# A two-layer bidirectional encoder trunk: the global branch's output projection trails its gates by four feature tiles instead of three, and some attention steps move half a product earlier

## The chip, the cores and the metric

One Trainium2 (trn2) chip, one core. The metric is the device time of one execution in microseconds (us); it covers the whole trunk, from the load of the first activations to the last store. The kernel before took 846.28 us in the median of 3 runs (844.58 to 846.31). PE is TensorE, DVE is VectorE, ACT is ScalarE, POOL is GpSimd, SP is SyncE, which issues the loads.

## The reference

Two layers over 528 tokens (16 meta tokens and a grid of 8 rows of 64), width 1024. Each layer normalises the residual stream, projects it once, and runs two attentions on parts of the projection: a global one (GQA, 8 query heads on 2 key/value heads of 64) and a windowed one (NA, 8 heads, an 8 x 16 window with a learned bias and the meta keys). Each branch is gated, projected to the width, and the two are merged by sigmoid gates:

```python
def hybrid_layer(x, norm_g, w_in, q_norm_g, k_norm_g, rpb, w_o_attn, w_o_na, w_out, cos, sin):
    b, l, _ = x.shape
    h = rms_norm(x, norm_g)
    proj = jnp.einsum('bld,de->ble', h, w_in)
    qa, ka, va, za, qb, kb, vb, zb, ga, gb = split_cols(proj)
...
    oa = gqa_attention(qa, ka, va) * jax.nn.silu(za)
...
    ob = neighbourhood_attention(qb, kb, vb, rpb) * jax.nn.silu(zb)

    ya = jnp.einsum('ble,ed->bld', oa, w_o_attn)
    yb = jnp.einsum('ble,ed->bld', ob, w_o_na)
    mixed = jax.nn.sigmoid(ga) * ya + jax.nn.sigmoid(gb) * yb
    return x + jnp.einsum('bld,de->ble', mixed, w_out)
```

After the second layer the meta tokens are dropped.

## The kernel before, in words

Activations are kept transposed: features on the partitions, tokens along the free dimension, in 8 feature tiles. Every product is made in three passes over split operands (`product`, L325 to L327): weights and activations are each held as a rounded part (`hi`, fp32r) and the remainder (`lo`), and hi x hi, hi x lo and lo x hi are summed in a PSUM bank, named `pp` for a projection and `y` for the output projection of a branch. In layer 0 a product of one feature tile has two halves of 264 columns, 24 matmuls each; in layer 1 most have one half of 512 columns.

Weights stream in chunks of 512 columns: `weights` (L229 on) issues the load `raw` on SP, the cast `whi` on ACT (L240) and the remainder `wlo` on POOL (L241), four buffers of each, in the sequence of the list `order` (L207 to L220), three chunks ahead of their use. A chunk's name is layer, number, half: GA (26 to 33) are the gates of the global branch, GB (34 to 41) those of the window branch, WOA (42 to 45) and WOB (46 to 49) the branches' output projections, and 50 on the final one.

The two attentions run beside the projections. Each has a queue, `Side`, that `product` advances by a tick after each half product (in layer 1 also in the middle of one). A unit (GQA: one query head for two blocks of 128 queries, each with scores S of its own, so 16 units; `av_7_1` is the last) or a head (NA) may start at each fourth tick; its steps are then due so many ticks later, by the tables `GQA_AT` and `NA_AT`. In these, "split" are the two casts `pth` (ACT) and subtractions `ptl` (DVE) of a unit's transposed probabilities, which the matmuls `av` (L905) then read; "stages" are six steps of a head: preparation, scores Sb (L556, L557; reduced on DVE at L990), first transpositions ta and tm, second transpositions tb, third tc, and sums avb. "values" are two transpositions of the window's values, the second named vtc; they belong to the even heads, one for each pair. `split` (L190) makes hi and lo of a tile: `tah` and `tal` of ta, `oa_3a` and `oa_3b` of the gated output oa_3 of the global branch's last feature tile.

PSUM buffers: two for `pp` and `y`, two for transpositions (tag tp: ta, tb, tc, tm, vtc), and a single one of two banks, S, for scores of both attentions: the unit's scores (reduced at L837) and the window's Sb.

What is due at a tick is written into the instruction streams at that place; a scheduler then orders each engine's stream by its own priorities and the dependences, which is why the built order is read below.

After all projections come the merges. `merge_gate` makes a gate tile (L1131, L1132), `merge_half` the output projection of a branch (L1137 multiplies it by the gate). In the loop over m the product of tile m - LAG follows the gate of tile m, first for GB and WOB, then for GA and WOA; in the second loop the two branches are added (L1170) and split into `mx`. At m = LAG - 1 `side_gqa.finish()` (L1166) runs the ticks of the queue that are still open, since the product after it reads the last `oa`. In layer 1 the loop also starts the splits of the final weights (`last_split`, POOL L272).

Of the kernel before, what the change touches and what calls it, by code (L numbers as in the profile page):

```python
# [33 lines left out]
DEPTH = 2  # L34


GQA_AT = ({"scores": (0, 1), "turn": (1, 2), "back": 3, "split": (5, 5), "ends": 5, "divide": (2, 3, 6), "sums": (7, 7)},
          {"scores": (0, 1), "turn": (1, 2), "back": 3, "split": (5, 5), "ends": 5, "divide": (2, 3, 6), "sums": (7, 7)})
NA_AT = ({"stages": (0, 2, 5, 5, 5, 7), "values": (3, 4), "divide": (3, 4, 7)},
         {"stages": (0, 2, 4, 5, 5, 7), "values": (3, 4), "divide": (3, 4, 7)})  # L40

NORM_AT = ({"tokens": (0, 1, 3), "squares": (1, 1, 2, 3, 2), "heads": (2, 3, 5, 7, 6), "values": (1, 4)},
# [4 lines left out]
QA, KA, VA, ZA, QB, KB, VB, ZB, GA, GB = 0, 4, 5, 6, 10, 14, 18, 22, 26, 34  # L47
WOA, WOB, WOUT = 42, 46, 50
NCHUNK = 58

LAG = 3

# [41 lines left out]
def trunk_kernel(ctx: ExitStack, tc: tile.TileContext, xT, w, gn, gf, bias, rope, out):  # L96
    nc = tc.nc
# [15 lines left out]
    def slot(tag, name, dt=F32):  # L113
        n = NKEY if tag in ("KB", "KR", "K", "E") else NTOK
        t = slots.tile([P, n], dt, tag=tag, bufs=BUFS[tag], name=name)
        return t[:, :NTOK] if tag == "E" else t
# [90 lines left out]
    order = []  # L207
    for l in range(DEPTH):
        cols = [QA, QA + 1, QA + 2, QA + 3, KA, VA]
        for j in range(4):  # L210
            cols += [KB + j, QB + j, VB + j, ZB + j, ZA + j]
        order += [(l, c, i) for c in cols for i in range(2)]
        if l == 0:

            order = order[6:]
        for gate, wo in ((GB, WOB), (GA, WOA)):
            for m in range(8 + LAG):
                order += [(l, gate + m, 0), (l, gate + m, 1)] if m < 8 else []
                order += [(l, wo + (m - LAG) // 2, (m - LAG) % 2)] if m >= LAG else []
        order += [(l, WOUT + m, i) for m in range(8) for i in range(2)] if l < DEPTH - 1 else []  # L220
    place = {key: i for i, key in enumerate(order)}
    ready, loaded = [], []
# [44 lines left out]
    def last_split(us):  # L267
        for u in us:
            hi, lo = (((key_half if tag == "KB" else lambda name, dt: slot(tag, name, dt))(f"wl{u}{tag}", F32R))[:, :4 * P]
                      for tag in ("h", KEEP[u]))  # L270
            cast = nc.scalar.copy(hi, last_raw[u])
            sub = nc.gpsimd.tensor_sub(lo, last_raw[u], hi.bitcast(F32))  # L272
            split_at["weights"] = cast.ins, sub.ins
            last_w[u] = hi, lo

    l = 0
# [157 lines left out]
    first, ends = {}, ((0, HALF), (HALF, NTOK))  # L434
# [19 lines left out]
    for l in range(DEPTH):  # L454
        last = l == DEPTH - 1
# [135 lines left out]
        qs, turn = [], None  # L591
        for j in range(4):
# [3 lines left out]
            with tc.issue_after(evac["low"].ins):  # L596
                if l == 0 and j == 0:
                    turn = rotate
                else:
                    if turn:  # L600
                        turn()
                    turn = None
# [224 lines left out]
        zgate, oa, o_t, newest, sums_a = {}, [None] * 4, {}, {}, {}  # L827
# [19 lines left out]
        def global_unit(kv, parts, n, name, done):  # L847
# [7 lines left out]
            def scores(i):  # L855
                q, qs, scale, total = parts[i]
                if i == 0:
                    c["both"] = slots.tile([P, 2 * NTOK], F32, tag="M", bufs=BUFS["M"], name=f"P{name}")
                    c["p"] = [c["both"][:, NTOK * t:NTOK * (t + 1)] for t in range(len(parts))]
                softmax(c["p"][i], q, qs, kv, NMETA - first_token[i], n, scale, total, f"{name}_{i}")  # L860

            def turn(i):

                a, b = (0, NREAL) if i == 0 and len(parts) > 1 else (NREAL * i, NREAL * i + NREAL + 32)
                if len(parts) == 1:
                    nc.gpsimd.memset(c["both"][:n, NTOK:b], 0.0)
                nc.vector.transpose(c["both"][:n, a:b], c["both"][:n, a:b])  # L867
                if i == len(parts) - 1:
                    c["there"] = dpool.tile([P, 2 * (NREAL + 32)], F32, tag="turned", bufs=3, name=f"turn{name}")
                    nc.sync.dma_start(c["there"][:n, :b], c["both"][:n, :b])  # L870
# [30 lines left out]
            def sums(first, last):  # L901
                if first == 0:
                    c["av"] = bank(ps_a, f"av{name}", "avg")[:, :width]
                for i in range(first, last):
                    nc.tensor.matmul(c["av"], rows2(c["t"][i][0]), c["t"][i][1], start=i == 0, stop=i == 8)  # L905
                if last == 9:
                    done(c["av"])

            steps = [(at, lambda i=i: scores(i)) for i, at in zip(range(len(parts)), GQA_AT[l]["scores"])]
            for i, at in zip(range(len(parts)), GQA_AT[l]["turn"][-len(parts):]):  # L910
                steps.append((at, lambda i=i: turn(i)))
            steps.append((GQA_AT[l]["back"], back))
            n_t = 4 // per
            for i, (at, then) in enumerate(zip(GQA_AT[l]["split"][:n_t], GQA_AT[l]["sums"][-n_t:])):
                steps.append((at, lambda kt=per * i: split_part(kt)))
                f = 2 * per * (i + 1)
                steps.append((then, lambda a=2 * per * i, b=f + (f == 8): sums(a, b)))
            steps.append((GQA_AT[l]["ends"], split_ends))
            return sorted(steps, key=lambda x: x[0])
# [26 lines left out]
        def start_unit(hd, i):  # L946
# [6 lines left out]
            if g == 6:  # L953
                steps += zip(GQA_AT[l]["divide"], divided_later(sums_a[j], lambda: zgate[j], f"a{l}_{j}"))
            return sorted(steps, key=lambda x: x[0])
# [135 lines left out]
        def start_head(hd):  # L1091
            steps = list(zip(NA_AT[l]["stages"], windowed_head(hd)))
            j = hd // 2
            if hd % 2 == 0:
                steps += [(at, lambda i=i: window_values(j, i)) for i, at in enumerate(NA_AT[l]["values"])]
                kvq[j]["sums"] = tiny.tile([P, 8], F32, tag="sumb", name=f"sumb{l}_{j}")
            else:
                steps += zip(NA_AT[l]["divide"], divided_later(kvq[j]["sums"], lambda: zb[j], f"b{l}_{j}"))
            return sorted(steps, key=lambda x: x[0])
# [35 lines left out]
        def merge_half(m, t, c, br, out, spans=None):  # L1135
            for ps, a, b in product(l, c + m // 2, br, full, (m % 2,), f"y{m % 2}", spans):
                nc.vector.scalar_tensor_tensor(out[:, a:b], t[:, a:b], 1.0, ps, op0=ALU.add, op1=ALU.mult)  # L1137
                yield a, b

        mb, gates = [], {}  # L1140
        for m in range(8 + LAG):
            if m < 8:
                gates[m] = merge_gate(GB, m)
            if m == LAG - 1:
                side_na.finish()
                while ending:
                    ending.pop(0)()
            if m >= LAG:
                mb.append(slot("B", f"mb{l}_{m - LAG}"))
                for _ in merge_half(m - LAG, gates[m - LAG], WOB, ob, mb[m - LAG]):  # L1150
                    pass
        mixed = []
        for m in range(8 + LAG):
            if m < 8:
                gates[m] = merge_gate(GA, m)
            if last and m == 7:

                weights(l, WOA + 3, 1, 1)
                with tc.issue_after(split_at["gate"].ins):
                    last_split((0, 1, 2))  # L1160
            if m == LAG - 1:
                side_gqa.finish()
            if m >= LAG:
                ma = slot("G", f"ma{l}_{m - LAG}")
                hi, lo = two("M", f"mx{l}_{m}", F32R)
                end = m == 7 + LAG  # L1166
                for a, b in merge_half(m - LAG, gates[m - LAG], WOA, oa, ma):
                    if (end and full) or b == N:
                        a = a if end else 0
                        nc.vector.tensor_add(ma[:, a:b], ma[:, a:b], mb[m - LAG][:, a:b])  # L1170
                        with ExitStack() as held:
                            if last and m in (7, 8):
                                held.enter_context(tc.issue_after(split_at["weights"][0]))
                            split(hi[:, a:b], lo[:, a:b], ma[:, a:b])
                mixed.append((hi, lo))
                if last and m in (7, 8):
                    with tc.issue_after(split_at["hi"].ins):
                        last_split(((3, 4, 5), (6, 7))[m - 7])
            if last and m == 4:
                last_load(range(KT))  # L1180

# [37 lines left out]
    sums = tiny.tile([P, 50], F32, tag="mh", bufs=1, name="sums")  # L1219
    acc, ms, rx = sums[:, :12].rearrange("p (t i) -> p t i", i=3), sums[:, 12:16], sums[:, 16:20]  # L1220
    h2 = D // 4
    for f in range(2):
        for t in range(4):
            x = xs[f, t]
            end = f == 1 and t == 3
# [89 lines left out]
```

## Time and profile before

| | us |
|---|---|
| median of 3 runs | 846.28 (844.58 to 846.31) |
| the profiled execution | 845.68 |
| its span in the profile | 844.0 |
| PE busy | 821.0 (97%) |
| DVE, ACT, POOL busy | 522.8, 474.8, 422.8 |
| mean granted clock | 0.996 |

The span is the time between the profile's first and last instruction, 1.7 us less than the execution's own time. A matmul's busy time overlaps with that of the next, so that the distance of two starts tells what one costs. A wait is put down to the line and tile that released it.

### The profile page before, as it was taken

To read this page: it belongs to the slowest core of one execution; us is meant where nothing else is said; L and a number is where in the kernel's file an instruction comes from. 1 tells how busy PE (TensorE), PEld (TensorE's weight loads), DVE (VectorE), ACT (ScalarE), POOL (GpSimd) and SP (SyncE) were. 2 spreads that over 40 slices of the span, in tenths; PEclk is the share of its full clock that TensorE was granted. 3 is DMA by queue.
4 is the path that set the end of the run, shared out by engine and by line. 5 is a ranking of instruction groups with operands and counts; after the bars stand their busy time and mean duration, and the time that the engine had idled before them with its cause. 6 is when DMAs were issued, how large, how long until landed. Compare 5 with 4: busy or idle time off the path is not lost.

```text
span 844.0 us, 16154 instructions
## 1 busy us (share of the span) xinstructions
PE 821.0 (97%) x5662; PEld 757.9 (90%) x5662; DVE 522.8 (62%) x1152; ACT 474.8 (56%) x1137; POOL 422.8 (50%) x362
## 2 busy tenths in 40 slices
PE   9999999999999999899999999999999999999997
PEld 9999999999999999899998989898988787778786
DVE  7976667676765562436547656766776556545633
ACT  8654766667864563333445456675768545543422
POOL 1664545444444453654764644444545436464851
PEclk9999999999999999999999999999999999999999
DMA  7277564667454664335555585647566566444502
GB/s 277 89 195 223 133 196 116 197 195 197 147 161 118 188 178 128 108 93 150 151 141 121 152 212 154 196 160 225 153 187 197 167 193 187 140 147 140 185 3 101
DMA packets 113249, 135.00 MB, mean 160 GB/s; under 512 B 31888, under 2 KB 66192, under 8 KB 113168
## 3 DMA queue, kind: packets, MB, share of 16 engines
q1 hardware_dynamic: 112448, 132.90, 54.0%
q8 instruction: 45, 0.74, 0.4%
q10 hardware_dynamic: 720, 1.06, 0.3%
q14 instruction: 36, 0.29, 0.1%
HBM read 98.50 MB, written 21.84 MB: 143 GB/s over the span
## 4 chain that ended last, share of the span: by engine, by line
PE 85%; DVE 6%; ACT 3%; issue 2%; DMA 2%; SPq 1%; POOL 0%; POOLq 0%; DVEq 0%; ACTq 0%
PE pp L327 18%; PE pp L325 18%; PE pp L326 18%; PE av L905 4%; PE y L326 3%; PE y L327 3%; PE y L325 3%; DVE ptl L194 2%; PE avb L1052 2%; PE S L556 2%; PE S L557 2%; PE pf L1234 2%; PE pf L1236 2%; PE pf L1235 2%; PE tb L129 1%
## 5 line engine op out<-in xcount | busy, mean ns | idle before, releaser
L241 POOL TENSOR_TENSOR wlo<-raw,whi 128x512 fp32r<-128x512 f32 x210 | 287.5, 1376 | 322.2 <-ACT whi L240 262.1
L327 PE MATMUL pp<-hh,wlo 128*128 128x264 f32 (+3 forms) x1040 | 325.8, 313 | 0.6 <-POOL wlo L241 0.6
L325 PE MATMUL pp<-hh,whi 128*128 128x264 f32 (+3 forms) x1040 | 326.1, 314 | 0.3 <-DVE ma L1137 0.3
L326 PE MATMUL pp<-hl,whi 128*128 128x264 f32 (+3 forms) x1040 | 324.0, 312 | 0.0
L327 PEld LDWEIGHTS pp<-hh,wlo 128*128 128x128 f32 x1040 | 196.4, 189 | 11.2 <-POOL wlo L241 0.8
L326 PEld LDWEIGHTS pp<-hl,whi 128*128 128x128 f32 x1040 | 196.8, 189 | 9.5
L325 PEld LDWEIGHTS pp<-hh,whi 128*128 128x128 f32 x1040 | 196.2, 189 | 9.5 <-DVE ma L1137 0.5
L240 ACT CAST whi<-raw 128x512 fp32r<-128x512 f32 x210 | 128.7, 618 | 116.5 <-PE pp L326 41.4
L867 DVE STREAM_TRANSPOSE P<-P 128x512 f32<-128x512 f32 x64 | 46.4, 726 | 38.9 <-ACT P L841 38.6
L898 POOL TENSOR_TENSOR ga<-pm,ga 32x128 fp32r<-32x128 f32 x64 | 40.4, 632 | 47.9 <-issue 26.8
L194 DVE TENSOR_TENSOR ptl<-P,pth 128x512 fp32r<-128x512 f32 x64 | 55.6, 881 | 12.8 <-ACT pth L193 10.3
L1131 DVE TENSOR_TENSOR mg<-pp,rbc 128x264 f32<-128x264 f32 (+1 forms) x48 | 24.7, 515 | 50.2 <-PE pp L327 49.5
L837 DVE CUSTOM_DVE_ANT_1 P<-S,r 128x528 f32<-128x528 f32 x64 | 44.8, 700 | 14.5 <-PE S L557 13.7
L841 ACT ACTIVATE P<-P,st 128x528 f32<-128x528 f32 x64 | 47.1, 737 | 1.7
L1132 ACT ACTIVATE mg<-mg 128x264 f32<-128x264 f32 (+1 forms) x48 | 23.7, 493 | 36.9 <-DVE mg L1131 36.8
L193 ACT CAST pth<-P 128x512 fp32r<-128x512 f32 x64 | 39.2, 612 | 1.4 <-DMA P<-turn 1.3
L905 PE MATMUL av<-ptl,VA 128*128 128x256 f32 x128 | 35.0, 299 | 4.1 <-DVE ptl L194 3.7
L992 ACT ACTIVATE bias<-bias,stb 128x208 f32<-128x208 f32 (+1 forms) x64 | 31.0, 486 | 13.3 <-DVE stb L990 13.2
L326 PE MATMUL pp<-mx,whi 128*128 128x264 f32 x128 | 36.6, 286 | 0.0
L327 PE MATMUL pp<-mx,wlo 128*128 128x264 f32 x128 | 36.4, 284 | 0.0
L325 PE MATMUL pp<-mx,whi 128*128 128x264 f32 x128 | 36.3, 284 | 0.0
L840 ACT ACTIVATE st<-st 128x1 f32<-128x1 f32 x64 | 13.0, 202 | 40.9 <-DVE st L837 40.5
(534 smaller groups left out, 1727.4 us busy)
## 6 DMA issues: line engine op xcount, KB each, us to landing
raw<-in_w_dram SPq DMA_DIRECT2D x210, 256.0 KB
turn<-P SPq DMA_DIRECT2D x32, 528.0 KB
P<-turn SPq DMA_DIRECT2D x128, 128.0 KB
bias<-in_bias_dram SPq DMA_DIRECT2D x16, 480.0 KB
KB<-KB SPq DMA_DIRECT2D x24, 272.0 KB
rawl<-in_w_dram SPq DMA_DIRECT2D x16, 256.0 KB
x<-in_xT_dram SPq DMA_DIRECT2D x8, 264.0 KB
xr<-in_xT_dram SPq DMA_DIRECT2D x8, 264.0 KB
```

Source lines behind the costliest of these rows:

```text
L193: split_at["hi"] = nc.scalar.copy(hi, src)
L194: split_at["any"] = nc.vector.tensor_sub(lo, src, hi.bitcast(F32))
L240: cast = nc.scalar.copy(hi, raw)
L241: sub = nc.gpsimd.tensor_sub(lo, raw, hi.bitcast(F32))
L325: nc.tensor.matmul(ps, wh, rh[:, a:b], start=i == 0, stop=False)
L326: nc.tensor.matmul(ps, wh, rl[:, a:b], start=False, stop=False)
L327: nc.tensor.matmul(ps, wl, rh[:, a:b], start=False, stop=i == n - 1)
L837: newest["max"] = nc.vector.tensor_tensor_reduce(p[:n].rearrange("p (i k) -> p i k", i=2), S[:n, :, :HALF], scale[:n].unsqueeze(2).to_broa ...
L841: nc.scalar.activation(p[:n], p[:n], AF.Exp, bias=st[:n, 1:2], scale=1.0, accum_out=st[:n, 2:3] if total is None else total)
L867: nc.vector.transpose(c["both"][:n, a:b], c["both"][:n, a:b])
L898: nc.gpsimd.tensor_sub(tm[64 + 32 * t:96 + 32 * t, n * t:n * (t + 1)], m, tm[:32, :n].bitcast(F32))
L905: nc.tensor.matmul(c["av"], rows2(c["t"][i][0]), c["t"][i][1], start=i == 0, stop=i == 8)
```

## The change

The first table entry that differs is "split" of both layers: the first of a unit's two splits is due at tick 4, not 5. The second is "stages" of layer 0: the first transpositions ta and tm are due at tick 4, not 5, as they already were in layer 1. The third is a lag of its own, LAG_A = 4, for the global branch's merge: `order`, the loop bound, the place of `side_gqa.finish()`, and the indices under which the final weights are split follow it; the latter keep their place against the products of WOA.

```diff
-GQA_AT = ({"scores": (0, 1), "turn": (1, 2), "back": 3, "split": (5, 5), "ends": 5, "divide": (2, 3, 6), "sums": (7, 7)},
-          {"scores": (0, 1), "turn": (1, 2), "back": 3, "split": (5, 5), "ends": 5, "divide": (2, 3, 6), "sums": (7, 7)})
-NA_AT = ({"stages": (0, 2, 5, 5, 5, 7), "values": (3, 4), "divide": (3, 4, 7)},
+GQA_AT = ({"scores": (0, 1), "turn": (1, 2), "back": 3, "split": (4, 5), "ends": 5, "divide": (2, 3, 6), "sums": (7, 7)},
+          {"scores": (0, 1), "turn": (1, 2), "back": 3, "split": (4, 5), "ends": 5, "divide": (2, 3, 6), "sums": (7, 7)})
+NA_AT = ({"stages": (0, 2, 4, 5, 5, 7), "values": (3, 4), "divide": (3, 4, 7)},
          {"stages": (0, 2, 4, 5, 5, 7), "values": (3, 4), "divide": (3, 4, 7)})
...
 LAG = 3
+
+LAG_A = 4
...
-        for gate, wo in ((GB, WOB), (GA, WOA)):
-            for m in range(8 + LAG):
+        for gate, wo, lag in ((GB, WOB, LAG), (GA, WOA, LAG_A)):
+            for m in range(8 + lag):
                 order += [(l, gate + m, 0), (l, gate + m, 1)] if m < 8 else []
-                order += [(l, wo + (m - LAG) // 2, (m - LAG) % 2)] if m >= LAG else []
+                order += [(l, wo + (m - lag) // 2, (m - lag) % 2)] if m >= lag else []
...
-        for m in range(8 + LAG):
+        for m in range(8 + LAG_A):
             if m < 8:
                 gates[m] = merge_gate(GA, m)
-            if last and m == 7:
+            if last and m == LAG_A + 4:
...
-            if m == LAG - 1:
+            if m == LAG_A - 1:
                 side_gqa.finish()
-            if m >= LAG:
+            if m >= LAG_A:
...
-                            if last and m in (7, 8):
+                            if last and m - LAG_A in (4, 5):
...
-                if last and m in (7, 8):
+                if last and m - LAG_A in (4, 5):
...
-                        last_split(((3, 4, 5), (6, 7))[m - 7])
+                        last_split(((3, 4, 5), (6, 7))[m - LAG_A - 4])
```

(In the lines left out of the loop's body, LAG becomes LAG_A.) In the changed kernel the lines behind the constant stand two further down: L325 becomes L327, L905 becomes L907.

What the built order makes of it is shown at three places. The first is PE's order in layer 0 at the last global unit, `av_7_1`; `y_42` is the first product of WOA, `pp_30` that of gate tile 4, `ga` the last operand of the unit. Before, the unit stands inside the first product of WOA:

```order
L327 MATMUL y_42_264_5189<-oa_2a,wlo_42_0_5104 128x264
L905 MATMUL av_7_1_5081<-pth_7_1_0_5041,VA_775 128x256
...
L905 MATMUL av_7_1_5081<-ga_120,VA_775 128x256
L325 MATMUL y_42_0_5175<-oa_3a,whi_42_0_5103 128x264
L325 MATMUL y_42_264_5189<-oa_3a,whi_42_0_5103 128x264
L326 MATMUL y_42_0_5175<-oa_3b,whi_42_0_5103 128x264
```

After the change it stands inside the gate product, and ACT's order at the same place (from `COPY` on) follows:

```order
L907 MATMUL av_7_1_5121<-ga_120,VA_775 128x256
L327 MATMUL pp_30_0_5180<-hh_4_190,whi_30_1_5090 128x264
L328 MATMUL pp_30_0_5180<-hl_4_191,whi_30_1_5090 128x264
L327 MATMUL pp_30_264_5207<-hh_4_190,whi_30_1_5090 128x264
L328 MATMUL pp_30_264_5207<-hl_4_191,whi_30_1_5090 128x264
L329 MATMUL pp_30_0_5180<-hh_4_190,wlo_30_1_5091 128x264
...
L771 COPY cmb_5132<-av_7_1_5121 64x256
L242 CAST whi_30_1_5090<-raw_30_1_5006 128x512
L242 CAST whi_42_0_5170<-raw_42_0_5012 128x512
L195 CAST oa_3a<-oa_3_3917 128x528
```

What reads `oa_3a` has moved 33 matmuls away from the unit's last; what now stands right behind it reads the weight chunk 30, second half, whose cast on ACT comes after the copy of the unit's output.

The second place is PE's order in layer 0 where head 4 of the window attention transposes; `S_3_0_1` are scores of a global unit. Before:

```order
L739 MATMUL vtc_2_2823<-ident,vb_2_2289 80x128 x3
L556 MATMUL S_3_0_1_2844<-KA0h_935,Q_1_679 128x264
L557 MATMUL S_3_0_1_2844<-KA0l_936,Q_1_679 128x264
...
L325 MATMUL pp_13_264_2854<-hh_0_143,whi_13_0_2654 128x264
L326 MATMUL pp_13_264_2854<-hl_0_144,whi_13_0_2654 128x264
```

After:

```order
L131 MATMUL ta_4_2827<-ident,bias_4_2600 128x128 x4
L131 MATMUL tm_4_2836<-ident,pm_126 32x128
L558 MATMUL S_3_0_1_2857<-KA0h_935,Q_1_679 128x264
L559 MATMUL S_3_0_1_2857<-KA0l_936,Q_1_679 128x264
...
L327 MATMUL pp_13_264_2867<-hh_0_143,whi_13_0_2654 128x264
L741 MATMUL vtc_2_2840<-ident,vb_2_2293 80x128 x3
L328 MATMUL pp_13_264_2867<-hl_0_144,whi_13_0_2654 128x264
```

Before, ta came a half product behind vtc; now ta and tm stand ahead of it, and vtc follows after four matmuls of scores and one of the projection.

The third place is PE's order in layer 1 at the window scores of head 1, `Sb_1`; `pp_11` is the projection running there. Before:

```order
L557 MATMUL Sb_1_7344<-KB_01_6908,QB_0b 128x208
L325 MATMUL pp_11_0_7331<-hh_4_6121,whi_11_1_7189 128x512
...
L327 MATMUL pp_11_0_7331<-hh_7_6342,wlo_11_1_7190 128x512
L1052 MATMUL avb_0_7386<-na_122,VB_0_7164 128x256
```

After:

```order
L559 MATMUL Sb_1_7382<-KB_01_6908,QB_0b 128x208
L327 MATMUL pp_11_0_7369<-hh_4_6121,whi_11_1_7224 128x512
...
L328 MATMUL pp_11_0_7369<-hl_6_6270,whi_11_1_7224 128x512
L558 MATMUL S_1_0_1_7409<-KA1h_6925,Q_0_6533 128x264
L559 MATMUL S_1_0_1_7409<-KA1l_6926,Q_0_6533 128x264
```

Eight matmuls of the projection behind the last of the window's scores now stand scores of a global unit, which before stood in another tick.

## Rows read from the trace of the kernel before

**Rows 1.** The page: the span, and shares of the chain that ended last by engine.

```profile
span 844.0 us, 16154 instructions
...
PE 85%; DVE 6%; ACT 3%; issue 2%; DMA 2%; SPq 1%; POOL 0%; POOLq 0%; DVEq 0%; ACTq 0%
```

**Rows 2.** What PE waited for: us in total, times, longest us.

```profile
PE tb L129 <- DVE tal L194: 3.5, 3, 1.5
...
PE y L326 <- DVE oa_3b L194: 1.1, 2, 0.6
```

**Rows 3.** PE's timeline in layer 0: start us, us, what, [idle before <-releaser].

```profile
338.59 0.28 PE L905 MATMUL av<-ga,VA 128*128 128x256 f32 x1
341.26 0.51 PE L325 MATMUL y<-oa_3a,whi 128*128 128x264 f32 x2 [2.39 <-ACT oa_3a L193]
...
346.34 0.29 PE L326 MATMUL pp<-hl,whi 128*128 128x264 f32 x1
346.46 0.28 PE L327 MATMUL pp<-hh,wlo 128*128 128x264 f32 x1
```

**Rows 4.** Stretches: us, busy PE, PEld, DVE, ACT, POOL, granted clock, DMA.

```profile
238.90:242.90 4.00, 2.49 (x22) 2.31 (x21) 2.75 (x5) 1.38 (x6) 2.66 (x2) 1.00 0.51 159
...
338.90:342.90 4.00, 1.12 (x6) 0.84 (x6) 2.20 (x4) 2.65 (x5) 3.75 (x3) 1.00 0.06 4
342.90:346.30 3.40, 3.12 (x15) 2.98 (x14) 2.67 (x4) 1.25 (x2) 3.40 (x3) 0.50 0.56 181
```

**Rows 5.** ACT's timeline at the same place.

```profile
338.90 0.36 ACT L769 COPY cmb<-av 64x256 f32<-64x256 f32 x1 [1.38 <-PE av L905]
339.29 1.14 ACT L240 CAST whi<-raw 128x512 fp32r<-128x512 f32 x2
```

**Rows 6.** The page's groups, the weight remainders: busy us, mean ns of one, idle.

```profile
L241 POOL TENSOR_TENSOR wlo<-raw,whi 128x512 fp32r<-128x512 f32 x210 | 287.5, 1376 | 322.2 <-ACT whi L240 262.1
```

**Rows 7.** POOL's timeline in the tail of layer 1.

```profile
784.99 1.30 POOL L272 TENSOR_TENSOR wl1K<-rawl,wl1h 128x512 fp32r<-128x512 f32 x1
786.24 1.74 POOL L272 TENSOR_TENSOR wl2K<-rawl,wl2h 128x512 fp32r<-128x512 f32 x1
```

**Rows 8.** PE's timeline at head 6 of the window attention, layer 0.

```profile
239.38 0.28 PE L326 MATMUL pp<-hl,whi 128*128 128x264 f32 x1
241.18 0.63 PE L129 MATMUL tb<-ident,bias 128*128 128x128 f32 x4 [1.51 <-DVE tal L194]
```

**Rows 9.** DVE's timeline at three places of layer 0.

```profile
129.55 0.70 DVE L837 CUSTOM_DVE_ANT_1 P<-S,r 128x528 f32<-128x528 f32 x1
...
240.35 0.68 DVE L194 TENSOR_TENSOR tal<-ta,tah 128x512 fp32r<-128x512 f32 x1
...
383.09 0.43 DVE L1137 SCALAR_TENSOR_TENSOR ma<-mg,y 128x264 f32<-128x264 f32 x1
```

**Rows 10.** PE's and DVE's timelines at the window scores of head 1, layer 1.

```profile
517.52 0.28 PE L557 MATMUL Sb<-KB,QB_0b 128*128 128x208 f32 x1
517.64 0.41 PE L325 MATMUL pp<-hh,whi 128*128 128x512 f32 x1
517.88 0.40 PE L326 MATMUL pp<-hl,whi 128*128 128x512 f32 x1
...
519.72 0.37 DVE L990 CUSTOM_DVE_ANT_0 bias<-Sb,bias 128x208 f32<-128x208 f32 x1
```

**Rows 11.** DVE's timeline in the tails of layer 0 and layer 1.

```profile
383.56 0.71 DVE L1170 TENSOR_TENSOR ma<-ma,mb 128x528 f32<-128x528 f32 x1
...
384.97 1.01 DVE L194 TENSOR_TENSOR mx<-ma,mx 128x528 fp32r<-128x528 f32 x1
...
785.29 1.55 DVE L1170 TENSOR_TENSOR ma<-ma,mb 128x512 f32<-128x512 f32 x1
...
788.46 0.67 DVE L1137 SCALAR_TENSOR_TENSOR ma<-mg,y 128x512 f32<-128x512 f32 x1
...
791.86 0.68 DVE L1137 SCALAR_TENSOR_TENSOR ma<-mg,y 128x512 f32<-128x512 f32 x1
...
797.74 0.69 DVE L194 TENSOR_TENSOR mx<-ma,mx 128x512 fp32r<-128x512 f32 x1 [0.69 <-ACT mx L193]
```

More of the change, by code (lines that the diff above doesn't have):

```diff
@@ L1160, in trunk_kernel @@
                     last_split((0, 1, 2))
-            if m == LAG - 1:
+            if m == LAG_A - 1:
                 side_gqa.finish()
-            if m >= LAG:
-                ma = slot("G", f"ma{l}_{m - LAG}")
+            if m >= LAG_A:
+                ma = slot("G", f"ma{l}_{m - LAG_A}")
                 hi, lo = two("M", f"mx{l}_{m}", F32R)
-                end = m == 7 + LAG
-                for a, b in merge_half(m - LAG, gates[m - LAG], WOA, oa, ma):
+                end = m == 7 + LAG_A
+                for a, b in merge_half(m - LAG_A, gates[m - LAG_A], WOA, oa, ma):
                     if (end and full) or b == N:
                         a = a if end else 0
-                        nc.vector.tensor_add(ma[:, a:b], ma[:, a:b], mb[m - LAG][:, a:b])
+                        nc.vector.tensor_add(ma[:, a:b], ma[:, a:b], mb[m - LAG_A][:, a:b])
                         with ExitStack() as held:
-                            if last and m in (7, 8):
+                            if last and m - LAG_A in (4, 5):
                                 held.enter_context(tc.issue_after(split_at["weights"][0]))
```

## The prediction

> **What bounds the kernel now.** The page comes first. TensorE (PE) is busy 97% of the 844.0 us span, and the chain that ended last is TensorE's for 85% [rows 1]. Making another engine faster is worth nothing here; only the places where PE stands still can be won or lost. The second view is therefore the list of what PE waited for [rows 2], of which tb for tal (3 waits) and y for oa_3b (one wait in each layer, the longer 0.6 us) bear on this change, and a wait of y for oa_3a that the timeline shows with its surroundings [rows 3]. The third view is that timeline, which prices these waits from one matmul's start to the next. In a row, 264-column matmuls start 0.12 us apart, as 346.34 and 346.46 show [rows 3]. What a changed order will make of the waits is worked out from the built order and these durations. The sum is made against the profiled execution, 845.68 us, which is 0.6 below the median of the three runs, 846.28. About 0.2%, 1.7 us, is what a measurement of this kernel can tell from no change.
>
> **Layer 0, the first global product (the lag): -3.15.** The last score-value matmul of the GQA branch starts at 338.59, and its output must become oa_3a before the first product of WOA can go on, at 341.26; the clock then falls, and is back at 346.34 [rows 3]. The stretch from 342.90 to 346.30 ran at a granted 0.50, the lower of the two levels, 1.2 GHz, after a stretch in which PE had mostly stood still [rows 4]. Whether the clock falls after a pause differs: around head 6's wait of 1.7, below, it stayed at 1.00, the upper level, 2.4 GHz [rows 4]. From 338.59 to 346.34 there are 20 matmul starts; 20 x 0.12 = 2.4, so 7.75 - 2.4 = 5.35 us are lost. With a lag of four, 33 matmuls (24 of the gate product and 9 of the WOA product on oa_0 to oa_2) stand ahead of the first that reads oa_3a: 33 x 0.12 = 4.0 us, against 341.26 - 338.59 = 2.7 needed. That wait goes.
>
> What is late next is the second weight chunk of the same gate product, whi_30_1. ScalarE's queue has its cast behind the copy of av into cmb, and that copy waits for PE: it starts 0.31 after the last av and takes 0.36, and a cast comes right behind it, 0.57 each (two in 1.14) [rows 5]. So whi_30_1 is there at 338.90 + 0.36 + 0.03 + 0.6 = 339.9, where PE wants it at 338.71: 1.2 us of waiting. Then PE has four matmuls (0.5 us) before wlo_30_1, which GpSimd makes in 1.38 us on average [rows 6]: a further 0.9. The splits of GpSimd in the tail, 1.30 and 1.74 [rows 7], bound this by 0.8 and 1.25. I take 1.2 + 1.0 = 2.2 and no fall of the clock, because the two pauses together are less than half of the old 5.35; if it falls, 1.6 more (in 342.90 to 346.30, 15 matmuls in 3.40 us [rows 4], 0.23 each in place of 0.12). Sum -5.35 + 2.2 = -3.15; ends -5.35 (no wait for whi_30_1) and -1.3 (1.25 for the second wait, and the clock).
>
> **Layer 0, transpositions half a product sooner: -1.0.** tb uses one of two banks, and waits until ta has been split. It comes one half product after ta, and in heads 2, 4 and 6 that is not enough. In head 6 the matmul before tb starts at 239.38 and tb at 241.18 [rows 8]: 1.8 - 0.12 = 1.7 lost. The three waits make 3.5 in the list [rows 2], and 4.0 by starts read in this way. A half product is 24 matmuls, 2.9 us, more than any of the waits. So 4.0 us are won.
>
> Against this, heads 2, 4 and 6 issue vtc, the transposition of the window's edge values, in the very tick into which ta and tm are moved, and vtc now takes the bank that ta has just filled. It waits for the same split. In head 2, 16 matmuls and four of the scores stand between (covered), in heads 4 and 6 only four of the scores and one other, 0.6 us. After ta ScalarE casts and VectorE subtracts; in front of that subtraction (0.68) stand, in head 6, a split of about the same size, a reduction of scores (0.70) [rows 9] and a multiply of 264 columns (0.43 [rows 9]), so 2.5 - 0.6 = 1.9 to 2.1; in head 4 only two small ones, so 0.75 to 1.0. Together 3.0 (1.5 if ScalarE and VectorE happen to be idle, 6 if all three heads wait as tb does). Net -4.0 + 3.0 = -1.0; ends -2.5 and +2.0.
>
> **The split at tick 4 instead of 5: 0.** In layer 0 the casts that make pth stand among the same rows of ScalarE's order as before, at most two weight casts sooner: the scheduler had already pulled them forward. What would be won is a part of the waits of av for ptl; with this order I count none of it.
>
> **Layer 1, the second consequence of the lag: +2.1.** side_gqa.finish() counts ticks on while something is due. A tick later, in layer 0, nothing is due, so it stops one count sooner, and in layer 1 the units of the GQA queue start at another phase: three ticks sooner, while the window heads stay. The second scores of a unit (S) now fall in the same tick as a head's window scores (Sb). Both use the single two-bank buffer. S must wait until VectorE has reduced Sb four times. The cover is eight 512-column matmuls: 0.24 apart, from the last Sb matmul at 517.52 that is 0.12 + 8 x 0.235 = 2.0 us [rows 10]. In head 1 the fourth reduction ended 519.72 + 0.37 - 517.52 = 2.57 us after the last Sb matmul [rows 10]; the eight heads of layer 1, each read in this way, have 1.70, 2.57, 1.70, 2.14, 3.37, 1.95, 8.29 and 1.83. Six heads (not 4 and 6) meet the short cover. With these ends the wait would be 0.6 and 0.15 in two heads, 0.75 in all; with a transposition and a reduction of scores, about 0.7 each, in front of the reductions in every head, 1.4 in each of six, 8.4 in all. I take 0.35 each, 2.1, nearer to the low end since most heads stand there.
>
> **Layer 1, end of the queue: -0.6.** With units three ticks sooner nothing is due when the global products begin, and the wait for oa_3b, 0.6 [rows 2], goes.
>
> **The tail of layer 1: +0.6.** Five WOA products in place of four now follow the last gate with nothing between. VectorE's round for one takes 791.86 - 788.46 = 3.40 us [rows 11], PE's product 12 x 0.235 = 2.8. The last mx (797.74 + 0.69) holds the final projection, so one more round that is too long costs 0.6. In the tail of layer 0 a round is 0.43 + 0.71 + 0.43 + 1.01 = 2.6 (a half, the add, a half, the split) [rows 9, 11], under PE's 24 x 0.12 = 2.9: nothing.
> The tail add takes 1.55 beside a split of GpSimd and 0.71 in the tail of layer 0 [rows 11]. The Trainium skill, "SBUF — State Buffer", section "SBUF: two separate sides", says that VectorE with two SBUF inputs and GpSimd reading SBUF exclude each other for a whole instruction; the trace agrees in kind, with 0.84 us more. By the rule alone the added round could be held for a whole split, 1.30, and the sum would be 1.3 higher.
>
> **The sum.** -3.15 - 1.0 + 0 + 2.1 - 0.6 + 0.6 = -2.05 on 845.68: **843.6 us**.
>
> **The rivals.**
> Slower: the shared score buffer decides. If VectorE stands behind one transposition and one reduction at each head, S waits 1.1 us for each of eight heads, 8.8 in place of 2.1: 845.68 - 2.05 + 6.7 = 850.3. For it speaks head 1's 2.57 and the strict order of VectorE; against it, that half of the heads end within the cover. It turns the sign from about 0.75 us per head on. Chance 0.20.
> No change: the two new weight waits drop the clock (+1.6) and vtc waits for as much as tb did (+1.0): 846.2. For it speaks [rows 4], where pauses of this kind ended at half clock; against it, that the one in head 6 did not [rows 4]. Chance 0.24.
> No change by a held tail: a split of GpSimd, 1.30 [rows 7], holds the added round: 844.9. For it speaks the add of 1.55 beside GpSimd, against it that the rounds after it repeat at 3.40. Chance 0.06.
> Faster by much: the scheduler's order leaves slack that I don't see, and none of the new waits appears: -5.35 - 4.0 - 0.6 + 0.6 = -9.35, 836.3; with half of the 7.3 us that I put on them, 840.0. Against it, that each new wait follows from rows. Chance 0.12.
> That the change doesn't do what it says holds for the split alone, and stands in the sum as 0.
>
> **How the numbers follow.** The forecast itself has 0.38. Of it 0.34 lies over 1.7 us below, 0.04 within. Faster is 0.34 + 0.12 + 0.02 of the no-change case = 0.48; same 0.04 + 0.17 + 0.05 = 0.26; slower 0.20 + 0.05 + 0.01 = 0.26. The range goes from 838.5, the far end of the clean case left out, to 849.5, short of the full price of the collision. The forecast's own range is 841 to 846.
>
> **What would show it.** In the list of waits, y for oa_3a is gone, pp for whi and wlo at about 340 us of some 2 us stands in its place; tb for tal is gone, vtc for tal stands at heads 4 and 6 with 2 and 1 us; in layer 1 S for the reduction of Sb, six times, some 0.3 each. The granted clock of the stretch after 342 is 1.00. The forecast is wrong if S waits over 0.75 us per head, or if the new weight wait is as long as the old one.

## The result, and the profile after

The changed kernel takes 837.9 us in the median (834.92 to 838.6, 4 runs) against 845.88 of the kernel before on the same chip (4 runs): a ratio of 0.9905, 95% interval [0.9883, 0.9927], some 8 us. The forecast was 843.6, and the time lies 0.6 us below its range (838.5 to 849.5). The profiled execution took 838.60 us with a span of 836.8, 7.2 less than before. The number of matmuls is the same, 5662; added up from the starts of the matmuls, PE's pauses of over 0.06 us beyond the usual distance fell from 37.6 to 30.3 us.

The list of what PE waited for in the changed kernel answers to [rows 2] (us in total, times, longest):

```profile
PE av L907 <- DVE ptl L196: 2.9, 5, 1.0
PE pp L329 <- POOL wlo L243: 2.1, 3, 1.0
PE vtc L741 <- DVE tal L196: 1.7, 2, 1.3
PE S L558 <- DVE stb L992: 1.2, 2, 0.8
...
PE pp L327 <- ACT whi L242: 1.1, 1, 1.1
```

The waits of tb for tal and of y for oa_3a and oa_3b are gone; vtc for tal, pp for whi and wlo and S for stb (the reduction of Sb) are the new waits that the forecast had named, though vtc's are not at the heads that it gave. Compared by layer the list says more. In layer 1 (490 to 805 us) the kernel before had

```profile
PE av L905 <- DVE ptl L194: 3.2, 6, 0.8
PE y L325 <- ACT ob L193: 1.5, 1, 1.5
PE avb L1052 <- DVE na L798: 0.9, 1, 0.9
PE y L326 <- DVE oa_3b L194: 0.6, 1, 0.6
```

and the changed kernel has, in the same layer (470 to 800 us),

```profile
PE av L907 <- DVE ptl L196: 1.9, 3, 1.0
PE S L558 <- DVE stb L992: 1.2, 2, 0.8
PE pp L329 <- POOL wlo L243: 0.6, 1, 0.6
```

Two waits that no term of the forecast names, y for ob and avb for na, are gone, and av waits less.

Setting the starts of the same products in both traces side by side gives the place of the 7 us. At the end of gate product 29 of layer 0 the changed kernel is 3.0 us ahead, behind the last product of WOA in layer 0 4.7, at the first attention step of layer 1 4.6, at the last product of WOA in layer 1 7.5, and at the end 7.0. So 4.7 come from layer 0 and 2.4 from layer 1, where a net loss of 2.1 us was forecast (2.1 - 0.6 + 0.6). Some of layer 0's lead is a matter of the one profiled execution: the lag alone and the shift alone, two kernels of the next section whose layer 0 is unchanged up to this point, also stand 1.1 and 0.7 us ahead of the profile before at gate product 29.

At the first global product of layer 0 PE's timeline answers to [rows 3]:

```profile
335.79 0.28 PE L907 MATMUL av<-ga,VA 128*128 128x256 f32 x1
337.16 0.40 PE L327 MATMUL pp<-hh,whi 128*128 128x264 f32 x1 [1.09 <-ACT whi L242]
...
338.92 0.53 PE L329 MATMUL pp<-hh,wlo 128*128 128x264 f32 x1 [1.00 <-POOL wlo L243]
```

The two pauses are those forecast: 1.26 and 1.16 us by starts, for 1.2 and 1.0. The clock fell after them, which the forecast had as its less likely case (stretches, with the columns of [rows 4]; the granted clock is the third number from the end):

```profile
334.90:339.00 4.10, 2.01 (x15) 1.59 (x14) 1.91 (x4) 2.73 (x6) 3.62 (x4) 1.00 0.01 2
339.00:342.40 3.40, 3.40 (x16) 3.40 (x17) 0.86 (x2) 0.87 (x2) 3.40 (x3) 0.50 0.48 130
```

### The profile page after: what moved, and what is told of

Same layout as the page of the kernel before. It is cut to its first block, busy times and chain, and to the rows that moved or that the text cites. A ratio compares the mean times of both kernels' runs of the same rounds, so it can differ in the third digit from the quotient of the medians.

```text
span 836.8 us, 16152 instructions
## 1 busy us (share of the span) xinstructions
PE 818.4 (98%) x5662; PEld 757.9 (91%) x5662; DVE 524.8 (63%) x1152; ACT 473.8 (57%) x1137; POOL 423.0 (51%) x362
## 3 DMA queue, kind: packets, MB, share of 16 engines
q10 hardware_dynamic: 720, 1.06, 0.3%
## 4 chain that ended last, share of the span: by engine, by line
PE 76%; DVE 8%; DMA 5%; ACT 4%; issue 3%; SPq 2%; POOL 1%; POOLq 0%; DVEq 0%; ACTq 0%
PE pp L329 17%; PE pp L327 16%; PE pp L328 16%; PE av L907 4%; PE y L329 3%; PE y L328 3%; PE y L327 3%; PE pf L1236 2%; DMA turn<-P 2%; PE pf L1238 2%; PE S L559 2%; PE pf L1237 2%; PE S L558 2%; DMA bias<-in_bias_dram 1%; PE avb L1054 1%
## 5 line engine op out<-in xcount | busy, mean ns | idle before, releaser
L327 PE MATMUL pp<-hh,whi 128*128 128x264 f32 (+3 forms) x1040 | 326.8, 314 | 1.1 <-ACT whi L242 1.1
L327 PEld LDWEIGHTS pp<-hh,whi 128*128 128x128 f32 x1040 | 196.4, 189 | 10.0 <-ACT whi L242 1.3
L900 POOL TENSOR_TENSOR ga<-pm,ga 32x128 fp32r<-32x128 f32 x64 | 43.9, 686 | 63.4 <-ACT ga L898 31.4
L196 DVE TENSOR_TENSOR ptl<-P,pth 128x512 fp32r<-128x512 f32 x64 | 59.0, 933 | 9.5 <-ACT pth L195 8.1
L907 PE MATMUL av<-ptl,VA 128*128 128x256 f32 x128 | 34.1, 294 | 3.0 <-DVE ptl L196 2.9
L327 PE MATMUL pp<-mx,whi 128*128 128x264 f32 x128 | 36.4, 285 | 0.0
L907 PE MATMUL av<-pth,VA 128*128 128x256 f32 x128 | 34.5, 291 | 0.0
```

Source lines behind the costliest of these rows:

```text
L196: split_at["any"] = nc.vector.tensor_sub(lo, src, hi.bitcast(F32))
L327: nc.tensor.matmul(ps, wh, rh[:, a:b], start=i == 0, stop=False)
L900: nc.gpsimd.tensor_sub(tm[64 + 32 * t:96 + 32 * t, n * t:n * (t + 1)], m, tm[:32, :n].bitcast(F32))
```

## The experiments

All ratios are to the kernel before, timed beside it on the same chip. The changed kernel's own ratio is from another series of runs, and its interval reaches 1.9 us to either side; a difference of 2 us to it is therefore no proof by itself, and the parts are run alone on the kernel before as well. Theory A: the eight microseconds are the lag in layer 0, the transpositions in layer 0, and the shift of the GQA units against the heads in layer 1, which saves more than the collision on the score buffer costs. Theory B: the split at tick 4 shortened av's waits.

**Undoing the shift.** Layer 1's units start where they did before. The first pair of numbers is the GQA queue's starting tick in each layer, taken modulo four. Because the queue now stops one count sooner in layer 0, 3 is the old place in the changed kernel, 2 one tick sooner than that and 0 three; in the kernel before, 1 is three ticks sooner.

```diff
-GQA_AT_TICK, NA_AT_TICK = (0, 0), (1, 1)
+GQA_AT_TICK, NA_AT_TICK = (0, 3), (1, 1)
```

> The changed kernel, but the units of the GQA queue in layer 1 start at the tick of the kernel before again (the phase of that queue in layer 1 set from 0 to 3). Theory A, the phase: the 3 ticks by which these units start sooner took away waits of layer 1 that the forecast did not price (y for ob 1.66, avb for na 1.03, oa_3b 0.81 and part of av for ptl by starts) and cost 1.55 (S for Sb's reduction); undoing it gives back about 2.5 to 3 us: ratio to the kernel before about 0.994 in place of 0.9905, and the wait of y for ob is there again. Theory B, the split: the split at tick 4 shortened av's waits in layer 1, and the phase is worth at most 0.5 us: ratio 0.990 to 0.991. Forecast on record: the phase costs 1.5 us net (collision 2.1 less 0.6), so undoing it would win 1.5: ratio 0.989.

Measured: 839.06 us, ratio 0.9930 [0.9917, 0.9943], 0.0025 above the changed kernel's, or 2.1 us, a little under what theory A gave. The intervals of the two overlap, but the run with the split put back (below), which was timed together with this one, has 0.9902 [0.9889, 0.9915] and doesn't reach this one's. Theory B would have left it at 0.991, and the forecast's sign of this term is wrong. Both waits are back:

```profile
PE y L327 <- ACT ob L195: 1.5, 1, 1.5
...
PE avb L1054 <- DVE na L800: 0.9, 1, 0.9
```

This run also answers the question of the clock: its two pauses in layer 0 are 1.26 and 1.17 us, as in the changed kernel, and the stretch behind them ran at full clock, with 28 matmuls instead of 16 in 3.40 us:

```profile
338.00:341.40 3.40, 3.40 (x28) 3.40 (x29) 1.34 (x3) 1.70 (x4) 3.40 (x3) 1.00 0.41 133
```

So the same pauses sometimes drop the clock and sometimes don't. The fall costs about 1.5 us (12 matmuls of 0.12). The six runs of this kernel fall into two groups, 837.3 to 838.1 us at a mean clock of 0.999 and 840.0 to 840.6 at 0.997 to 0.998, which fits a fall in half of them; it may also be a part of the 3.7 us between the four runs of the changed kernel, whose mean clocks go from 0.996 (838.6) to 0.999 (834.92).

**The shift alone,** on the kernel before:

```diff
-GQA_AT_TICK, NA_AT_TICK = (0, 0), (1, 1)
+GQA_AT_TICK, NA_AT_TICK = (0, 1), (1, 1)
```

> The kernel before, with nothing changed but the phase of the GQA queue in layer 1 (0 to 1), so that its units start three ticks sooner, as in the changed kernel. Theory A: 2.5 to 3 us faster, ratio 0.9965 to 0.997; y for ob, avb for na and y for oa_3b in layer 1 go, S for the reduction of Sb comes with about 1.5 us. Theory B: within 0.5 us of the kernel before. The forecast's term: 1.5 us slower, ratio 1.002.

Measured: 842.39 us, ratio 0.9969 [0.9959, 0.9979], 2.6 us faster, as theory A had it, where the forecast's term was 1.5 us slower. One number in a table of phases gives a third of the change's gain. In its trace y for ob and avb for na are gone, and the collision is larger than in the changed kernel, three waits for 2.7 us:

```profile
PE S L556 <- DVE stb L990: 2.7, 3, 1.4
```

This trace is of the slowest of its eight runs, 845.18 us; half clock lasted 6.8 us in its layer 0, twice as long as in the profile before, and the gain is to be read from the median.

**The split back at tick 5:**

```diff
-"split": (4, 5)
+"split": (5, 5)
```

> The changed kernel with the first split of a unit due at tick 5 again in both layers. Theory A and the forecast: the split at tick 4 is worth nothing, within 0.6 us of the changed kernel, ratio 0.990 to 0.9915. Theory B: av's waits for ptl, which fell from 6.5 to 4.4 us by starts, come back: 2 us slower than the changed kernel, ratio 0.993.

Measured: 837.29 us, ratio 0.9902 [0.9889, 0.9915], the changed kernel's. Theory B falls; that part of the change does nothing, as forecast. The order changes all the same: in its trace vtc waits once, S for stb 0.4 in place of 1.2, and avb for na 0.8 is there again. That av waits less in layer 1 belongs to the shift: with the shift alone av waits 2.4 us in all, with the lag alone 3.7, as before the change.

**The first transpositions of layer 0 back at tick 5:**

```diff
-NA_AT = ({"stages": (0, 2, 4, 5, 5, 7), "values": (3, 4), "divide": (3, 4, 7)},
+NA_AT = ({"stages": (0, 2, 5, 5, 5, 7), "values": (3, 4), "divide": (3, 4, 7)},
```

> The changed kernel with the first transpositions of layer 0 due at tick 5 again. From the traces, by starts: the three waits of tb for tal (4.0) and of tm for VB (0.5) come back, two waits of vtc for tal (2.0) and one of avbm for tbl (0.8) go: 1.7 to 2.5 us slower than the changed kernel, ratio 0.9925 to 0.9935. The forecast's term was 1.0. If the order of layer 0 gives the time back elsewhere, within 0.5 us: ratio 0.990 to 0.991.

Measured: 838.68 us, ratio 0.9927 [0.9915, 0.9940], 1.9 us slower than the changed kernel by the ratios, and 2.1 slower than the run with the split back, which was timed with it. The time is as expected, the waits are not: vtc's are gone, but tb waits for tal only twice, for 1.3 us in all, where three waits with 4.0 were to come back, and S for stb in layer 1, which the edit doesn't touch, has grown from 1.2 to 2.0. The trace, of the slowest of the five runs, is 1.5 us behind the changed kernel's at gate product 29 of layer 0 and loses 1.0 more in layer 1.

**The same part alone,** the opposite line on the kernel before:

```diff
-NA_AT = ({"stages": (0, 2, 5, 5, 5, 7), "values": (3, 4), "divide": (3, 4, 7)},
+NA_AT = ({"stages": (0, 2, 4, 5, 5, 7), "values": (3, 4), "divide": (3, 4, 7)},
```

> The first transpositions of layer 0 at tick 4 alone, on the kernel before. Theory A: 1.9 us as when it was taken out of the changed kernel, ratio 0.9975 to 0.998; vtc waits for tal in heads 0 and 2 (1.5 and 0.5), not in heads 4 and 6. The forecast's term, 1.0 us: 0.9988, with vtc waiting in heads 4 and 6.

Measured: 843.42 us, ratio 0.9980 [0.9971, 0.9988]: 1.7 us. In its list vtc waits once, for 1.3 us, and a wait of tm for a DVE step that belongs to another head has come with 1.0, so that the new waits fall in heads 0 and 2 as in the changed kernel, but in head 2 it is tm that waits and not vtc. The forecast's heads, 4 and 6, have none.

**The lag alone:** the changed kernel with the tables of the kernel before, and with phase 3, so that the units of layer 1 start where they did.

```diff
-"split": (4, 5)
+"split": (5, 5)
...
-NA_AT = ({"stages": (0, 2, 4, 5, 5, 7), "values": (3, 4), "divide": (3, 4, 7)},
+NA_AT = ({"stages": (0, 2, 5, 5, 5, 7), "values": (3, 4), "divide": (3, 4, 7)},
...
-GQA_AT_TICK, NA_AT_TICK = (0, 0), (1, 1)
+GQA_AT_TICK, NA_AT_TICK = (0, 3), (1, 1)
```

> The lag of four alone: both tables as in the kernel before, and the phase of the GQA queue in layer 1 set so that its units start where they did before. Theory A (the parts add up): the changed kernel's 7.9 us less the phase's 2.1 to 2.65 and the transpositions' 1.9 leave 3.3 to 3.9 us for the lag: ratio 0.9954 to 0.9962. The forecast's terms for it, -3.15 - 0.6 + 0.6: 0.9963. Rival D, the changed kernel's own profile: 2.4 us of new waits and the clock's fall after them leave only 1.5 to 2 us: ratio 0.9975 to 0.998, and the parts would not add up.

Measured: 842.54 us, ratio 0.9967 [0.9954, 0.9979], 2.8 us by the ratio. It stands between the sum of the parts (3.3 to 3.9) and rival D (1.5 to 2); the interval holds all of A's range and only the edge of D's. The five runs tell more than their median: three have 842.5 to 842.7 us at a mean clock of 0.997 to 0.998, two 840.8 to 841.0 at 0.999 to 1.000. Against 844.69 for the kernel before, whose 15 runs all have 0.994 to 0.997, the first are 2.1 us faster, close to rival D, and the second 3.8, theory A. The profiled one is of the first kind and had 3.4 us of half clock from 340.7 us on. So the lag is worth some 2 or nearly 4 us, by whether the clock falls. The three parts alone give 0.9967 x 0.9969 x 0.9980 = 0.9916, within the changed kernel's interval: as closely as these intervals tell, the parts add up.

**A swap of two ScalarE instructions.** In the changed kernel the cast of whi_30_1 is ordered ahead of the copy of the last unit's output (an ordering of ScalarE alone, around the tick that emits the copy):

```diff
-            tick()
+            with ExitStack() as held:
+                if (l, c) == (0, GA + 3):
+                    held.enter_context(tc.issue_after(split_at["weights"][0]))
+                tick()
```

> The changed kernel with one swap in ScalarE's order of layer 0: the cast of whi_30_1 stands ahead of the copy of the last unit's av. The wait of pp for whi (1.26) goes; wlo_30_1 still stands behind a multiply on GpSimd that ends 0.9 us after the last av, so its wait grows from 1.16 to 1.7 to 2.1: 0.3 to 0.7 us faster than the changed kernel, ratio 0.9895 to 0.990, if the clock falls as before; if one pause in place of two keeps the clock, 1.5 more, ratio 0.988.

Measured: 835.54 us, ratio 0.9888 [0.9873, 0.9903]. ScalarE's timeline shows the cast where it had stood idle, and PE's that one pause is left:

```profile
334.67 0.62 ACT L242 CAST whi<-raw 128x512 fp32r<-128x512 f32 x1
336.20 0.37 ACT L774 COPY cmb<-av 64x256 f32<-64x256 f32 x1 [0.91 <-PE av L910]
```

```profile
335.88 0.29 PE L910 MATMUL av<-ga,VA 128*128 128x256 f32 x1
336.00 0.28 PE L327 MATMUL pp<-hh,whi 128*128 128x264 f32 x1
...
338.15 0.39 PE L329 MATMUL pp<-hh,wlo 128*128 128x264 f32 x1 [1.50 <-POOL wlo L243]
```

The pause for wlo is 1.66 us by starts, so the swap itself saves 2.42 - 1.66 = 0.8; the medians differ by more. This profile has no half clock in layer 0, and in the four runs the mean clock was 0.998 to 1.000; so the rest may be the clock's, and the ratio lies between the two that were expected. The two kernels were timed in different series of runs, though, and their intervals overlap.

**Another phase.** Units one tick sooner than before the change, not three:

```diff
-GQA_AT_TICK, NA_AT_TICK = (0, 0), (1, 1)
+GQA_AT_TICK, NA_AT_TICK = (0, 2), (1, 1)
```

> The changed kernel with the units of the GQA queue in layer 1 one tick sooner than in the kernel before, not three (phase 2 in place of 0); no unit's scores then stand directly behind a head's. If the collision is the only price of the phase and any earlier start takes the waits for ob and na away: the 1.55 us of S for Sb's reduction go, and the ratio is 0.988 to 0.989. If three ticks are needed for those waits to go, they come back (2.7 us): ratio 0.9915 to 0.993.

Measured: 836.58 us, ratio 0.9905 [0.9891, 0.9918], neither of the two. The collision is gone and av waits for ptl only 1.4 us, but the wait of y for ob is there, longer than before:

```profile
PE y L327 <- ACT ob L195: 2.0, 1, 2.0
```

It looks like the old wait, but what stood ahead of it is something else. ScalarE's cast followed VectorE's ob at once, VectorE waited for the gate zb, and GpSimd's zb for a DMA:

```profile
659.66 0.62 ACT L195 CAST ob<-ob 128x512 fp32r<-128x512 f32 x1 [1.40 <-DVE ob L779]
658.93 0.69 DVE L779 TENSOR_TENSOR ob<-ob,zb 128x512 f32<-128x512 f32 x1 [0.22 <-POOL zb L824]
657.63 1.27 POOL L824 TENSOR_TENSOR zb<-zb,sumsb 128x512 f32<-128x512 f32 x1 [1.12 <-DMA sumsb<-thereb]
```

In this profile the half clock came behind it, not in layer 0.

**Swap and phase 2 together.** The edits of both.

> The swap of the cast (as in e9_cast_first) with phase 2 in layer 1 (as in e11_phase2). If the parts add up: the swap's 1.3 us on top of phase 2's result, ratio 0.9885 to 0.9895; y for ob stays with about 2 us.

Measured: 833.78 us, ratio 0.9862 [0.9849, 0.9874], the fastest of all, below the changed kernel's whole interval and somewhat better than the parts; its profile has no half clock inside the work.

**The window's values sooner,** on top of the swap, in layer 0:

```diff
-"values": (3, 4)
+"values": (2, 3)
```

> The swap of the cast, and the window's value transpositions of layer 0 a tick sooner (2 and 3 in place of 3 and 4), so that vtc no longer stands in the tick of ta and tm. If vtc's wait for ta's split is what this part of the change still costs, its 1.4 and 0.5 us in heads 0 and 2 go: ratio 0.9863 to 0.987. If VectorE's queue at those places is simply late and another transposition waits for it, no change: 0.9885.

Measured: 836.99 us, ratio 0.9903 [0.9887, 0.9919], against 0.9888 with the swap alone: no gain. vtc's waits for tal are gone, and others of the same two banks have taken their place:

```profile
PE tc L131 <- DVE mm L1025: 0.8, 1, 0.8
PE tm L131 <- DVE VB L196: 0.8, 1, 0.8
```

**A lag of four for the window branch too,** with two phases (0 and 1), on top of the swap:

```diff
-LAG = 3
+LAG = 4
```

> The swap of the cast, and a lag of four for the window branch's merge too (GB and WOB). The heads in layer 1 then also start at another tick, and a unit's second scores stand a tick ahead of the window's scores. If a lag keeps y from waiting for the last output of its branch and the collision on the score buffer goes with the new phase: 1.5 us less than the swap alone, ratio 0.987. If new waits for weights appear at the last head, as they did at the last global unit in layer 0: 0.989 to 0.991.

> The same with the units of layer 1 one tick later (phase 1): the distance of a unit's second scores to the window's scores is then a half product shorter. If the phase of units against heads decides layer 1, this differs from phase 0 by over 1 us (0.987 against 0.9885 or the other way); if the last outputs decide it, both are equal within 0.5 us.

Measured: 853.13 us, ratio 1.0104 [1.0088, 1.0119], and 854.56 us, 1.0106 [1.0091, 1.0120]: some 9 us slower than the kernel before by the ratios, worse than either expectation. The loss is in layer 0, where units now follow each other with nothing between, each waiting for the single score buffer, and PE drops to half clock for a long stretch (phase 0; the list of waits, then stretches):

```profile
PE S L561 <- DVE st L842: 5.9, 6, 1.2
```

```profile
243.00:263.00 20.00, 14.71 (x104) 13.08 (x102) 13.82 (x35) 12.24 (x35) 6.68 (x7) 0.92 0.38 118
263.00:283.00 20.00, 13.08 (x48) 10.96 (x49) 13.19 (x27) 10.41 (x28) 4.51 (x5) 0.50 0.56 179
```

Why the scheduler packed them so was not followed further. What these two runs were to tell about ob and the phase they don't.

## Why the prediction was wrong

**The step that failed** is "Layer 1, the second consequence of the lag: +2.1". The shift of three ticks was found, and so was its price: S waits for the reduction of Sb, 0.56 and 0.98 us by starts in two heads, 1.5 together where 2.1 was put. But only the collision was priced. The shift moves every step of the units against every step of the heads, and of these the waits that were there before, y for ob (1.66 by starts), avb for na (1.03) and a part of av for ptl (3.2 to 1.9 in the lists above), should have been read as well: what stands ahead of them in their queues, and whether it still does.

For ob the trace shows it. Before, ScalarE copied the output of a unit ahead of the cast of ob, and that copy waited for PE:

```profile
666.49 0.37 ACT L769 COPY cmb<-av 64x256 f32<-64x256 f32 x1 [3.77 <-PE av L905]
666.76 0.62 ACT L240 CAST whi<-raw 128x512 fp32r<-128x512 f32 x1
667.28 0.62 ACT L193 CAST ob<-ob 128x512 fp32r<-128x512 f32 x1
```

ob itself had been ready on VectorE at 665.08 + 0.69 = 665.77, and PE, whose matmul before started at 666.18, went on at 667.95:

```profile
665.08 0.69 DVE L777 TENSOR_TENSOR ob<-ob,zb 128x512 f32<-128x512 f32 x1 [1.72 <-POOL zb L822]
667.95 0.50 PE L325 MATMUL y<-ob,whi 128*128 128x512 f32 x1 [1.50 <-ACT ob L193]
```

With the units three ticks sooner that copy comes 2.7 us ahead of the cast, and PE has no pause:

```profile
659.34 0.37 ACT L771 COPY cmb<-av 64x256 f32<-64x256 f32 x1
661.49 0.62 ACT L242 CAST whi<-raw 128x512 fp32r<-128x512 f32 x1 [1.78 <-POOL zb L824]
662.01 0.61 ACT L195 CAST ob<-ob 128x512 fp32r<-128x512 f32 x1
```

The two runs of the shift measured it from both sides: 2.1 and 2.6 us of gain, where the forecast had 2.1 less the 0.6 of oa_3b, a loss of 1.5. That the copy ahead of ob made the wait is read from the trace; no run swaps that pair by itself. What stood ahead of na and ptl was not followed, so for these waits the cause stays open.

**The other steps.** The lag in layer 0, -3.15: by the side-by-side starts -4.7 + 3.0 = -1.7 in this profile, with the clock's fall; in the profiles with the same order and no fall in layer 0, those of the shift undone and of phase 2, -3.4 and -3.2. The mechanism and both new waits were right, and whether the clock falls differs from run to run.

The transpositions, -1.0: 1.7 to 1.9 in the two runs; the mechanism was right and the size was not. (The 3.0 by gate product 29 hold about 1 us that isn't theirs, as said above.) One reading was of the wrong head, without harm to the sum: the wait of tb at 241.18, called head 6's in [rows 8], comes after the scores Sb of 3b, layer 0's last head, and is head 7's. Head 6's tb didn't wait:

```profile
221.57 0.66 PE L129 MATMUL tb<-ident,bias 128*128 128x128 f32 x4
223.42 0.26 PE L556 MATMUL Sb<-KB,QB_3b 128*128 128x208 f32 x1
```

The new waits of vtc were put into heads 4 and 6, with 3.0 us, because vtc was taken to follow into ta's bank there; they came in heads 0 and 2, with 1.45 and 0.53, while in heads 4 and 6 vtc started at once, as soon as the two small steps that read tm were done and with tal still to come. Head 6 of the changed kernel:

```profile
215.00 0.17 DVE L1022 TENSOR_TENSOR mm<-tm,mm 32x16 fp32r<-32x16 f32 x1
215.31 0.50 PE L741 MATMUL vtc<-ident,vb 128*80 128x128 f32 x3
216.97 0.68 DVE L196 TENSOR_TENSOR tal<-ta,tah 128x512 fp32r<-128x512 f32 x1
```

In each of the four heads vtc started 0.05 to 0.14 us behind whichever ended first, ta's split or tm's second step. How late the split would be was forecast well: it ended 0.7 us (head 4) and 2.3 us (head 6) after vtc's start, for 0.75 to 1.0 and 1.9 to 2.1. The bank was what the forecast had wrong.

The first split, 0: right. The end of the queue, -0.6: the wait went. The tail of layer 1, +0.6: the lead falls from 7.46 at the last product of WOA to 7.15 at the first matmul of the final projection and to some 7.05 behind its first group, so 0.3 to 0.4. The longer time by a held tail was weighed with the Trainium skill's "SBUF — State Buffer", section "SBUF: two separate sides". The trace agrees with its rule that the two engines exclude each other, and shows what it costs here: each of the five adds ends 0.55 us after the end of the split of GpSimd that was under way when it began. The first and the fourth add, each with the split beside it:

```profile
774.82 1.30 POOL L274 TENSOR_TENSOR wl1K<-rawl,wl1h 128x512 fp32r<-128x512 f32 x1
775.10 1.57 DVE L1172 TENSOR_TENSOR ma<-ma,mb 128x512 f32<-128x512 f32 x1
784.30 1.73 POOL L274 TENSOR_TENSOR wl4KB<-rawl,wl5h 128x512 fp32r<-128x512 f32 x1
785.51 1.06 DVE L1172 TENSOR_TENSOR ma<-ma,mb 128x512 f32<-128x512 f32 x1
```

The adds took 1.57, 1.07, 1.09, 1.06 and 1.08 us. All five are held, but four of them only for the last 0.5 us of a split, as in the rounds before the change, so that the added round costs no more than the others and the rival's 1.30 did not come.

**The rivals.** The time is that of the clean case (836.3 to 840.0), though not for its reason: it was given for new waits that fail to appear, and they came, with 2.4 us for weights, 2.0 for vtc and 1.5 for S. The gains that paid for them were in no case. The collision, the rival on the other side, exists, and decides nothing at two heads of six.

## What to carry to other kernels

When a change shifts one queue of steps against another, price every wait at which the two meet, those that may vanish as well as those that may appear; a list of the waits of the stage, each with what stands ahead of it in its engine's order, does it. Where an engine's stream has a fixed order, as ScalarE's here, a copy that waits for a late producer holds the ready work behind it (3.77 us of idle ScalarE at ob). One swap of such a pair was worth 0.8 us by the trace, and a few ticks of phase between two queues 2.1 to 2.6, about as much as the lag of the merge itself. Try the phases by themselves before paying for a longer lag: lag and phase are coupled here through the count at which the queue is drained.

## What the runs showed of the hardware

The same two pauses of PE, 1.26 and 1.16 us with four matmuls between, were followed by 3.4 us at a granted 0.50 in one profile and by full clock in another (the changed kernel and the one with the shift undone). A longer pause elsewhere (2.15 us by starts, phase 2) was followed by half clock at 660.4 us, and one of 2.43 us at the same place (swap and phase 2) was not (stretches behind the two pauses):

```profile
660.40:663.80 3.40, 3.40 (x8) 2.72 (x9) 1.88 (x4) 1.59 (x4) 0.00 (x0) 0.50 0.49 164
659.70:663.10 3.40, 3.40 (x15) 2.79 (x16) 2.48 (x5) 2.22 (x5) 0.62 (x1) 1.00 0.50 157
```

One execution's clock after a pause of this size is therefore no property of the kernel, and a difference of 1.5 us between two single profiles can be this alone.

GpSimd's splits hold up VectorE's adds of two 128x512 tiles: in the tails of layer 1, before and after the change, every such add that began during a split ended 0.55 us behind the split's end, whether 0.5 or 1.1 us of the split were left.
